# Seven-product FFN blocks: weight buffers, token order of the out projection, and the order of first tiles and products

## Chip, cores and metric

One core of one Trainium2 chip. The metric is the device time of one execution in microseconds (us), the median of several. TensorE is called PE here, VectorE DVE, ScalarE ACT, GpSimd POOL and SyncE SP.

## The reference

One decoder layer over 2048 prompt tokens and 64 sample tokens (8 sequences of 8), width 1024. What matters here is its second half:

```python
    mix = jnp.concatenate([oa, ob, oc, od], axis=-1).astype(dt) @ prm['w_out'][li]
    h = h + mix
    gu = rmsnorm(h, prm['norm2_g'][li]) @ prm['w_ffn_in'][li]
    h = h + (jax.nn.silu(gu[..., :D_FF]) * gu[..., D_FF:]) @ prm['w_ffn_out'][li]
    gate = jax.nn.sigmoid(rmsnorm(h, prm['ple_norm_g'][li]) @ prm['w_ple_gate'][li])
    h = h + (pl @ prm['w_ple'][li]) * gate
```

`D_FF` is 2816. `oa` to `od` are four token mixers (linear attention, dilated attention, gated delta rule, recurrent gates).

## The kernel before

The tokens are worked on in four blocks of 512 (`TB`); the 64 sample tokens ride with block 1 through the input projection and with block 3 through the rest, which then has 576 columns (`TBS`). A block has tiles 0 to 3 of 128 tokens; tile 4 is the 64 sample tokens, and the order of tiles is 0, 1, 4, 2, 3. Every product is done with operands split in two, a rounded part `hi` and a remainder `lo`, and three matmuls (hi hi, hi lo, lo hi) per 128 rows of contraction. A weight is loaded by SP into `wraw` (4 buffers), `hi` is cast on ACT into `whi` (7 buffers) and `lo` subtracted on DVE or POOL into `wlo` (7 buffers); `unit`, line 268 on, does this and alternates DVE and POOL.

Blocks 0 and 1 use `rest`, blocks 2 and 3 use `rest7` (line 596). `rest7` does the out projection (`out_mm`, line 434: four column quarters of 256, for each of them the tiles in turn), then `norm2`, then the FFN in `ffn7`, then the per-layer part (`per_layer_out`). The FFN runs over 22 row groups f of 128. Of a group, gate and up are computed together by a scheme of seven products of half the contraction, each over half of the block's tokens (256 columns, or 288 in block 3), instead of eight; `seven` (line 680) builds sums of weights on DVE, splits them (`parts`, lines 691 and 692), runs the products (`prod`, line 715) into three PSUM banks x, y and z, and combines them with DVE additions (line 696). The seven products are a11, s1, s2, a12, s3, s4, a22. The token operands are b11 and b21 (first half of the tokens), b22, and the differences t1 to t4; `Halves.steps` (line 121) transposes the normalized rows on PE (line 134), copies them out of PSUM scaled (`F`, lines 139 and 141) and splits the first half; `Halves.second` (line 153) makes the differences (line 164) and their splits. The first group, f = 0, is done by eight products, `mm_half` (line 670), half by half, since its first half needs only the first half of the tokens. FFN groups go in chunks of 1, 3, 3, ..., 3; after each chunk `out_mm` multiplies its gated values `g` with `w_ffn_out` (line 364, 512 columns) and adds to the residual rows `h` (line 582). The last chunk goes tile by tile, with the last norm's transposes (line 85) between.

The order of instructions on each engine is worked out when the kernel is built: a scheduler takes whatever is ready by its own modelled times, in order of a priority that counts up with the program text; `S.at(0)` puts something ahead of everything else. The sample tokens' mixers are given a higher priority than block 2 of `rest7` and run beside it. Pools of a new stage lie on memory of closed ones and wait tile by tile for it to come free. There are two pools of three PSUM banks for these products (`bank`), taken in turn.

## Time and profile before

| | us |
|---|---|
| median of three runs | 3446.8 |
| lowest and highest run | 3443.35, 3446.89 |
| profiled execution | 3437.55 |
| its span, first to last instruction | 3435.7 |
| PE busy in it | 3302.0 |
| DVE busy in it | 2254.7 |
| granted PE clock, mean | 0.978 |

The profile is of one execution. A row of the windows has, after the stretch and its length, the busy time (and instructions) of PE, its weight loads (PEld), DVE, ACT and POOL, then the granted clock as a share of full speed. Block 2's out projection ends in the stretch from 2346 to 2396 us, block 3's in that from 2910 to 2960, and block 3's work ends the span. A matmul's recorded time includes its way through the array, so the distance between starts is what one costs.

### The profile page before, as it was taken

Reading aid. Unit: us, or ns where it says so; the run is one execution under the profiler, and the core shown is the slowest. Engines: PE = TensorE matmul, PEld = TensorE weight load, DVE = VectorE, ACT = ScalarE, POOL = GpSimd, SP = SyncE. Lnnn points to the kernel's source line nnn. Section 1 sums busy time; section 2 is a strip of 40 time slices with the busy share of each in tenths; the row PEclk is TensorE's granted clock in tenths of the full one; section 3 lists DMA queues with packets and bytes.
Section 4 is the critical chain, followed back from the end, with each engine's and each line's share of the span. In section 5 each row is a group of like instructions: output and inputs, shape, how many; then the busy total and the mean of one; then the engine's idle time right before and its main releaser. Section 6 shows DMA issues by size and latency. Waiting matters only on the chain.

```text
span 3435.7 us, 66579 instructions
## 1 busy us (share of the span) xinstructions
PE 3302.0 (96%) x24742; PEld 2815.2 (82%) x24742; DVE 2254.7 (66%) x6002; ACT 1379.3 (40%) x2931; POOL 820.7 (24%) x696
## 2 busy tenths in 40 slices
PE   7999999999999999998999999999999999899998
PEld 6788997888887778788878776787888889788988
DVE  4455566544577756688775455446799875877875
ACT  4433445324344224345333334535343453433443
POOL 2212122122112222212122212122334432233431
PEclk9999999999999999999999999999999999999999
DMA  6645445544433332534432443463533344122222
GB/s 207 181 121 149 127 123 155 148 125 145 129 109 118 101 96 87 132 91 146 113 103 81 124 114 110 143 215 113 162 102 88 91 129 134 60 81 90 83 89 79
DMA packets 621769, 411.92 MB, mean 120 GB/s; under 512 B 155357, under 2 KB 572877, under 8 KB 621445
## 3 DMA queue, kind: packets, MB, share of 16 engines
q1 hardware_dynamic: 618184, 405.12, 40.8%
q8 instruction: 195, 3.19, 0.4%
q10 hardware_dynamic: 3260, 2.55, 0.3%
q14 instruction: 130, 1.06, 0.1%
HBM read 348.77 MB, written 61.18 MB: 119 GB/s over the span
## 4 chain that ended last, share of the span: by engine, by line
PE 72%; DVE 13%; DMA 6%; SPq 4%; issue 3%; ACT 2%; POOL 1%; DVEq 0%; ACTq 0%; POOLq 0%
PE mmp L364 25%; PE mmp L344 22%; PE mmp L715 9%; SPq L1321 2%; PE acc L1852 1%; DVE c_X L1312 1%; DVE c_tmp L1310 1%; DMA wraw<-w_ffn_in 1%; DVE wlo L283 1%; PE mx L1135 1%; PE mx L1707 1%; PE mmp L85 1%; PE mx L1653 1%; PE mx L1764 1%; PE mx L1047 1%
## 5 line engine op out<-in xcount | busy, mean ns | idle before, releaser
L283 POOL TENSOR_TENSOR wlo<-wraw,whi 128x512 fp32r<-128x512 f32 (+1 forms) x356 | 497.5, 1399 | 1763.0 <-ACT whi L280 1112.8
L344 PE MATMUL mmp<-act,whi 128*128 128x512 f32 (+1 forms) x2944 | 892.7, 384 | 7.6 <-ACT ev L368 5.0
L280 ACT CAST whi<-wraw 128x512 fp32r<-128x512 f32 (+1 forms) x712 | 436.4, 619 | 667.4 <-PE mmp L344 240.6
L344 PEld LDWEIGHTS mmp<-act,whi 128*128 128x128 f32 x2944 | 532.9, 190 | 111.9 <-ACT ev L368 6.8
L364 PE MATMUL mmp<-whi,act 128*128 128x256 f32 (+3 forms) x2992 | 574.8, 290 | 11.8 <-DVE act L297 6.9
L344 PE MATMUL mmp<-act,wlo 128*128 128x512 f32 (+1 forms) x1472 | 554.0, 383 | 0.0
L364 PE MATMUL mmp<-whi,g 128*128 128x512 f32 (+1 forms) x1496 | 491.2, 406 | 15.4 <-DVE h L492 5.8
L364 PEld LDWEIGHTS mmp<-whi,act 128*128 128x128 f32 (+1 forms) x2992 | 470.8, 190 | 21.5 <-DVE act L297 7.8
L364 PE MATMUL mmp<-wlo,act 128*128 128x256 f32 (+2 forms) x1496 | 431.0, 289 | 0.2 <-DVE wlo L283 0.2
L283 DVE TENSOR_TENSOR wlo<-wraw,whi 128x512 fp32r<-128x512 f32 (+1 forms) x356 | 279.9, 787 | 219.0 <-ACT whi L280 198.3
L692 POOL TENSOR_TENSOR wlo<-wraw,whi 128x512 fp32r<-128x512 f32 x168 | 243.6, 1453 | 468.6 <-ACT whi L691 411.8
L364 PEld LDWEIGHTS mmp<-whi,g 128*128 128x128 f32 (+1 forms) x1496 | 273.3, 188 | 95.5 <-ACT g L296 8.5
L715 PE MATMUL mmp<-Sb,whi 128*128 128x256 f32 (+1 forms) x1680 | 328.0, 292 | 7.2 <-DVE xs L696 5.8
L344 PEld LDWEIGHTS mmp<-act,wlo 128*128 128x128 f32 x1472 | 276.4, 190 | 50.2 <-issue 2.0
L364 PE MATMUL mmp<-wlo,g 128*128 128x512 f32 x748 | 297.6, 400 | 0.0
L364 PEld LDWEIGHTS mmp<-wlo,act 128*128 128x128 f32 (+1 forms) x1496 | 283.5, 190 | 4.0 <-issue 2.0
L715 PEld LDWEIGHTS mmp<-Sb,whi 128*128 128x128 f32 x1680 | 267.0, 190 | 12.7 <-DVE xs L696 8.4
L715 PE MATMUL mmp<-Sb,wlo 128*128 128x256 f32 (+1 forms) x840 | 241.7, 291 | 1.8 <-POOL wlo L692 1.8
L691 ACT CAST whi<-wraw 128x512 fp32r<-128x512 f32 x210 | 128.8, 619 | 229.1 <-PE mmp L364 94.5
L364 PEld LDWEIGHTS mmp<-wlo,g 128*128 128x128 f32 x748 | 140.2, 187 | 33.7 <-issue 0.5
L715 PEld LDWEIGHTS mmp<-Sb,wlo 128*128 128x128 f32 x840 | 159.0, 190 | 3.4 <-POOL wlo L692 2.2
L582 DVE TENSOR_TENSOR h<-mmp,h 128x512 f32<-128x512 f32 (+3 forms) x180 | 107.6, 630 | 72.0 <-PE mmp L364 65.5
(472 smaller groups left out, 5250.1 us busy)
## 6 DMA issues: line engine op xcount, KB each, us to landing
wraw<-w_ffn_in SPq DMA_DIRECT2D x352, 256.0 KB
wraw<-w_in SPq DMA_DIRECT2D x208, 256.0 KB
wraw<-w_ffn_out SPq DMA_DIRECT2D x176, 256.0 KB
wraw<-w_out SPq DMA_DIRECT2D x64, 256.0 KB
wraw<-w_ple_gate SPq DMA_DIRECT2D x64, 256.0 KB
bs_K<-cache_b_k SPq DMA_DIRECT2D x48, 256.0 KB
...
```

What stands on the lines that cost most here:

```text
L85: nc.tensor.transpose(ps[:, i * rows:(i + 1) * rows], s[:, k * 128:(k + 1) * 128], S.ident[:rows, :rows])
L280: nc.scalar.copy(hi, raw)
L283: eng.tensor_tensor(lo, raw, hi.bitcast(F32), op=ALU.subtract)
L344: nc.tensor.matmul(ps, u[a], acts[k][:, b, t:t + w], start=i == 0, stop=i == n)
L364: nc.tensor.matmul(ps, acts[k][:, b, t0:t0 + rows], units[k][a], start=i == 0, stop=i == n)
L582: nc.vector.tensor_tensor(d, ps, d, op=ALU.add)
L691: nc.scalar.copy(hi, x)
L692: eng.tensor_tensor(lo, x, hi.bitcast(F32), op=ALU.subtract)
L715: nc.tensor.matmul(ps, w[a][:, k], op[k][:, b], start=first and k == 0 and j == 0, stop=k == 3 and j == 2, skip_group_check=True)
L1047: nc.tensor.matmul(ss[:, k:k + 2], x[:, c, t * m:(t + 1) * m], M.blk2, start=True, stop=True)
L1135: nc.tensor.matmul(ps[64 * hp:64 * hp + ms, ct, n], k[r, ct, 64 * n:64 * n + ms], part(q[r, ct, 64 * n:64 * n + 64], 1), start=True, stop= ...
L1321: nc.sync.dma_start(out=xt[r, ct, n], in_=xd[:, hp, ct, n, d].rearrange("k j i -> j k i"))
```

## The change

In words, by function:

- `Halves`: the tokens lie in the order of the tiles, 0, 1, samples, 2, 3, so one copy instead of two takes a transposed group out of PSUM; half of these copies (k of 4 and more) go to DVE. The second group's transposes get the priority of their place in the text instead of the top one. `second` splits b12 and b22 of all k before it makes differences; the splits of t3 go to POOL. `F` shares its buffers with half of the differences (`Sf`).
- Weight parts come from further pools in turn with the old ones (`wparts`): 7 more in block 3, in the out projection and in the FFN each, 3 more in block 2's FFN. Sums of weights (`ws`) get 5 buffers in block 2.
- `out_mm` in block 3's out projection (`late`): the last two column quarters are done for tiles 0, 1 and 4 first, then both for tiles 2 and 3, with two steps of the norm after each of these products. `mid` gives the tiles their new place.
- `ffn7`: f = 0 and f = 1 are both done by halves, in the order first half of 0, second group of the norm, first half of 1, second half of 0, second half of 1. The chunks are 2, 3, 3, 3, 3, 3, 3, 2. The gated values are split in one piece.
- `seven`: the split of s1 comes later, s2 is split on DVE and a12 on POOL; the products go a11, s2, a12, s1, s3, s4, a22.

```diff
+    ORDER = (0, 4, 1, 5, 2, 6, 3, 7)
...
-        self.f = [fp.tile([128, 2 * self.w], F32, name="F") for _ in range(KT)]
+        self.f = {k: sf.tile([128, 2 * self.w], F32, name="F", tag="Sb") for k in self.ORDER}
...
-            for k in (0, 4, 1, 5, 2, 6, 3, 7):
-                with S.at(0):
+            for k in self.ORDER:
+                with S.at(S.tc.cur_priority if j else 0):
...
-                    t0 = j * w
-                    m = w if n > 256 else 256
-                    nc.scalar.mul(f[:, t0:t0 + m], ps[:, :m], g)
-                    if n > m:
-                        nc.scalar.mul(f[:, 2 * w - n + m:], ps[:, m:], g)
+                    g, f = self.gain[:, k:k + 1], self.f[k][:, t0:t0 + n]
+                    if k < 4:
+                        nc.scalar.mul(f, ps, g)
+                    else:
+                        nc.vector.tensor_scalar_mul(f, ps, g)
...
+            t0 += n
...
+        new = lambda p: p.tile([128, 2, w], F32R, name="Sb", tag="Sb")
+        for k in range(4):
+            S.split(self.b12[k], self.part(k, 1))
+            self.b22.append(new(sb))
+            S.split(self.b22[k], self.part(k + 4, 1))
         for k in range(4):
             b11, b12, b21, b22 = (self.part(a, j) for a, j in ((k, 0), (k, 1), (k + 4, 0), (k + 4, 1)))
-            d = sb.tile([128, 2, self.w], F32R, name="Sb")
-            self.b22.append(d)
-            S.split(d, b22)
             tmp = S.xsp.tile([128, D], F32, name="xs")
-            t1, t2, t3 = (tmp[:, i * self.w:(i + 1) * self.w] for i in range(3))
+            t1, t2, t3 = (tmp[:, i * w:(i + 1) * w] for i in range(3))
             sub(t1, b12, b11)
+            sub(t2, b22, t1)
             sub(t3, b22, b12)
-            sub(t2, b22, t1)
-            S.split(self.b12[k], b12)
-            sub(b21, b21, t2)
-            for n, x in (("t1", t1), ("t2", t2), ("t3", t3), ("t4", b21)):
-                d = sb.tile([128, 2, self.w], F32R, name="Sb")
-                self.t[n].append(d)
-                S.split(d, x)
+            for n, x in (("t1", t1), ("t2", t2), ("t3", t3), ("t4", t1)):
+                if n == "t4":
+                    sub(x, b21, t2)
+                self.t[n].append(new(sb if k < 2 else self.sf))
+                S.split(self.t[n][k], x, nc.gpsimd if n == "t3" else None)
...
+    def wparts(self):
+        self.nw += 1
+        _, hi, lo = self.wpools[self.nw % len(self.wpools)]
+        return hi, lo
...
+        hi, lo = self.wparts()
+        hi = hi.tile([128, nk, n], F32R, name="whi", tag="whi")
+        lo = lo.tile([128, nk, n], F32R, name="wlo", tag="wlo")
...
-            nc.vector.tensor_tensor(lo, src, hi.bitcast(F32), op=ALU.subtract)
+            (eng or nc.vector).tensor_tensor(lo, src, hi.bitcast(F32), op=ALU.subtract)
...
+        elif late:
+            def pairs():
+                for c in cols[:-2]:
+                    u = load(c)
+                    yield from ((c, i, u) for i in tiles)
+                us = [(c, load(c)) for c in cols[-2:]]
+                for part in (tiles[:-2], tiles[-2:]):
+                    yield from ((c, i, u) for c, u in us for i in part)
+            order = pairs()
...
-            use(i, c, self.mm_a(acts, u, nk, i * 128, NS if i == 4 else 128, n))
+            t0 = i * 128 if not mid or i < 2 else 256 if i == 4 else i * 128 + NS
+            use(i, c, self.mm_a(acts, u, nk, t0, NS if i == 4 else 128, n))
...
+            if late:
+                if not left[tiles[-3]] and i in tiles[-2:]:
+                    for _ in range(2):
+                        if steps < 8:
+                            norm.step()
+                            steps += 1
+            elif norm and not left[tiles[2]]:
...
-            ws, fp, sa = (ops.enter_context(pool(n, m)) for n, m in (("ws", 2), ("F", KT), ("Sa", KT)))
-            with pool("pad", 1) as pad, pool("W", KT) as wp:
-                if not with_s:
-                    pad.tile([128, 1400], F32, name="pad")
+            ws, sa, sf = (ops.enter_context(pool(n, m)) for n, m in (("ws", 2 if with_s else 5), ("Sa", KT), ("Sf", KT)))
+            @contextmanager
+            def weights(n):
+                with pool("whi2", n) as hi, pool("wlo2", n) as lo:
+                    own = self.wpools
+                    self.wpools = own + (own if n < 7 else []) + [(None, hi, lo)]
+                    yield
+                    self.wpools = own
+            with pool("W", KT) as wp, weights(7) if with_s else nullcontext():
                 self.actps, self.nacts = [wp], 0
                 acts = self.mixed(mix, smix)
                 for i, _ in self.tiles(with_s):
                     h[i] = self.load_x(self.hp.tile([128, D], F32, name="h"), b, i)
-                norm = Halves(self, h, self.gain["norm2_g"], with_s, fp, sa)
-                self.out_mm(acts, I["w_out"][0], KT, 256, with_s, add, norm)
-            last = self.ffn7(add, norm, ops.enter_context(pool("Sb", 20)), ws, with_s, w0)
+                norm = Halves(self, h, self.gain["norm2_g"], with_s, sa, sf)
+                self.out_mm(acts, I["w_out"][0], KT, 256, with_s, add, norm, late=with_s)
...
+            sb = ops.enter_context(pool("Sb", 12))
+            ops.enter_context(weights(7 if with_s else 3))
+            last = self.ffn7(add, norm, sb, ws, with_s)
...
+                self.out_mm(*last, 512, with_s, add, norm, True, mid=with_s)
...
+        def bank2(n):
+            if 2 * w0 > TB:
+                return [self.bank()[:, :w0] for _ in range(n)]
+            t = [self.bank() for _ in range((n + 1) // 2)]
+            return [t[i // 2][:, i % 2 * w0:(i % 2 + 1) * w0] for i in range(n)]
+        def glu(pairs):
+            th = self.ev.tile([128, TBS], F32, name="ev")
+            for j, (gate, up) in enumerate(pairs):
+                e = th[:, j * w0:(j + 1) * w0]
+                nc.scalar.activation(e, gate, AF.Tanh, scale=0.5)
+                nc.vector.scalar_tensor_tensor(e, e, 1.0, gate, op0=ALU.add, op1=ALU.mult)
+                nc.vector.scalar_tensor_tensor(e, e, 0.5, up, op0=ALU.mult, op1=ALU.mult)
+            g = self.gp.tile([128, 2, 2 * w0], F32R, name="g", tag="g")
+            self.split(g, th[:, :2 * w0])
+            return g
...
+        for n in (2, 3, 3, 3, 3, 3, 3, 2):
             gs = []
-            for f in range(f0, f0 + n):
-                wg, wu = (wi[:, c0:c0 + 128] for c0 in (f * 128, D_FF + f * 128))
-                th = self.ev.tile([128, TBS], F32, name="ev")
-                if f:
-                    pairs = self.seven(wg, wu, ops, ws, w0)
-                else:
-                    us = [self.units([w], KT, 4) for w in (wg, wu)]
-                    norm.first()
-                    pairs = []
-                    for j in range(2):
-                        if j:
-                            norm.second(sb)
-                        if w0 == 256:
-                            t = self.bank()
-                            ps = [t[:, :w0], t[:, w0:]]
-                        else:
-                            ps = [self.bank()[:, :w0] for _ in us]
-                        pairs.append([self.mm_half(p, u, norm.half(j)) for p, u in zip(ps, us)])
-                    ops = norm.operands(sb)
-                for j, (gate, up) in enumerate(pairs):
-                    e = th[:, j * w0:(j + 1) * w0]
-                    nc.scalar.activation(e, gate, AF.Tanh, scale=0.5)
-                    nc.vector.scalar_tensor_tensor(e, e, 1.0, gate, op0=ALU.add, op1=ALU.mult)
-                    nc.vector.scalar_tensor_tensor(e, e, 0.5, up, op0=ALU.mult, op1=ALU.mult)
-                g = self.gp.tile([128, 2, 2 * w0], F32R, name="g", tag="g")
-                gs.append(g)
-                halves = th[:, :2 * w0].rearrange("p (j n) -> p j n", j=2)
-                for c, m in ((0, 256), (256, w0 - 256)):
-                    if m:
-                        self.split(g[:, :, 2 * c:2 * (c + m)].rearrange("p a (j n) -> p a j n", j=2),
-                                   halves[:, :, c:c + m])
+            if not f0:
+                us = [[self.units([w], KT, 4) for w in cols(f)] for f in range(n)]
+                norm.first()
+                half = lambda f, j: [self.mm_half(ps, w, norm.half(j)) for ps, w in zip(bank2(2), us[f])]
+                pairs = [[half(0, 0)], []]
+                norm.second(sb)
+                pairs[1].append(half(1, 0))
+                for f in range(2):
+                    pairs[f].append(half(f, 1))
+                gs = [glu(p) for p in pairs]
+                ops = norm.operands()
+            gs += [glu(self.seven(*cols(f), ops, ws, w0)) for f in range(f0 + len(gs), f0 + n)]
             w = wo[f0 * 128:(f0 + n) * 128]
             f0 += n
             if f0 < FT:
-                self.out_mm(gs, w, n, 512, with_s, add)
+                self.out_mm(gs, w, n, 512, with_s, add, mid=with_s)
...
-        s1 = parts(s, V)
         tt(u1, g1, u1)
         tt(g1, s, g1)
-        s2 = parts(g1, G)
-        a12 = parts(g2, V)
+        s2 = parts(g1, V)
+        a12 = parts(g2, G)
+        s1 = parts(s, V)
...
-        x, z, y = (self.bank()[:, :w0] for _ in range(3))
+        x, y, z = (self.bank()[:, :w0] for _ in range(3))
         sv = self.xsp.tile([128, D], F32, name="xs")
         s, v, u = (sv[:, i * w0:(i + 1) * w0] for i in range(3))
         prod(x, a11, ops["b11"], True)
         nc.scalar.copy(s, x)
-        prod(z, s1, ops["t1"], True)
-        tt(v, z, s, ALU.add)
         prod(y, s2, ops["t2"], True)
         tt(u, y, s, ALU.add)
         prod(x, a12, ops["b21"], False)
+        prod(z, s1, ops["t1"], True)
+        tt(v, z, s, ALU.add)
```

## Rows read from the trace of the kernel before

**Rows 1.** The page's first part: busy time, share of the span and instructions of each engine.
```profile
PE 3302.0 (96%) x24742; PEld 2815.2 (82%) x24742; DVE 2254.7 (66%) x6002; ACT 1379.3 (40%) x2931; POOL 820.7 (24%) x696
```
**Rows 2.** Windows over stages: length, busy by engine, granted clock, DMA share, GB/s.
```profile
2346.00:2396.00 50.00, 42.89 (x382) 34.10 (x383) 37.22 (x100) 33.93 (x79) 5.90 (x4) 0.93 0.35 102
2396.00:2740.00 344.00, 328.68 (x2484) 288.07 (x2483) 289.42 (x600) 140.11 (x282) 136.53 (x97) 0.99 0.40 111
...
2910.00:2960.00 50.00, 37.20 (x222) 32.23 (x221) 44.06 (x118) 29.18 (x76) 6.35 (x5) 0.83 0.11 32
2960.00:3340.00 380.00, 376.22 (x2363) 337.68 (x2363) 293.84 (x460) 149.72 (x295) 143.24 (x103) 1.00 0.29 88
```
**Rows 3.** Windows over undisturbed matmuls of 288, 512 and 256 columns.
```profile
2961.00:2989.00 28.00, 28.00 (x213) 28.00 (x212) 22.54 (x38) 14.76 (x30) 14.26 (x11) 1.00 0.33 101
2999.50:3013.50 14.00, 13.85 (x60) 10.37 (x60) 9.90 (x16) 3.01 (x6) 3.68 (x3) 1.00 0.14 39
2810.00:2905.00 95.00, 94.86 (x804) 94.66 (x803) 49.13 (x114) 32.09 (x71) 22.78 (x16) 1.00 0.43 136
```
**Rows 4.** PE's waits, 2910 to 2960 us: total us, times, longest.
```profile
PE mmp L364 <- ACT g L296: 2.9, 1, 2.9
PE mmp L134 <- DVE xs L68: 2.8, 1, 2.8
PE mmp L676 <- DVE Sb L297: 2.8, 1, 2.8
PE mmp L134 <- ACT F L141: 2.7, 2, 2.5
```
**Rows 5.** Windows of 20 us in block 3's hand-over, columns as in the windows above.
```profile
2920.00:2940.00 20.00, 14.10 (x89) 13.07 (x90) 18.07 (x53) 15.41 (x46) 0.00 (x0) 0.74 0.05 14
2940.00:2960.00 20.00, 14.35 (x65) 11.43 (x64) 17.15 (x36) 6.76 (x16) 3.43 (x3) 0.83 0.14 39
```
**Rows 6.** Timeline, tile 3's rows from residual add to scaling: start us, us, engine.
```profile
2918.16 0.41 DVE L582 TENSOR_TENSOR h<-mmp,h 128x256 f32<-128x256 f32 x1
...
2922.55 1.14 ACT L313 ACTIVATE xs<-h 128x1024 f32<-128x1024 f32 x1
...
2927.51 0.75 DVE L68 TENSOR_SCALAR xs<-h,ss 128x1024 f32<-128x1024 f32 x1
```
**Rows 7.** Groups by line and shape, 2910 to 2960: busy us, mean ns | idle before.
```profile
L139 ACT ACTIVATE F<-mmp,gcol 128x288 f32<-128x288 f32 x8 | 3.7, 531 | 0.0
L164 DVE TENSOR_TENSOR xs<-F 128x288 f32<-128x288 f32 x8 | 3.5, 460 | 1.4 <-ACT F L139 1.4
```
**Rows 8.** PE's waits in block 2's FFN, 2396 to 2740 us.
```profile
PE mmp L715 <- DVE xs L696: 4.1, 7, 1.7
PE mmp L715 <- POOL wlo L692: 1.8, 2, 1.1
```
**Rows 9.** DVE's groups by line and shape in block 3's FFN, 2960 to 3340.
```profile
L696 DVE TENSOR_TENSOR ws<-wraw 128x512 f32<-128x512 f32 x39 | 47.3, 1214 | 18.3 <-DMA wraw<-w_ffn_in 18.1
L696 DVE TENSOR_TENSOR xs<-mmp,xs 128x288 f32<-128x288 f32 x105 | 46.1, 449 | 22.9 <-PE mmp L715 22.5
...
L696 DVE TENSOR_TENSOR wraw<-ws,wraw 128x512 f32<-128x512 f32 x20 | 13.6, 682 | 2.3 <-POOL wlo L692 2.2
...
L297 DVE TENSOR_TENSOR g<-ev,g 128x64 fp32r<-128x64 f32 x21 | 4.5, 213 | 0.0
```
**Rows 10.** PE's waits in block 3's FFN, 2960 to 3340.
```profile
PE mmp L364 <- DVE g L297: 1.9, 5, 0.4
...
PE mmp L715 <- DVE xs L696: 0.3, 1, 0.3
```
**Rows 11.** PE's waits at block 2's tail, 2770 to 2810.
```profile
PE mmp L85 <- DVE h L582: 3.2, 4, 1.7
PE mmp L364 <- DVE act L300: 1.6, 2, 1.4
```
**Rows 12.** POOL's group of weight splits, 2396 to 3340.
```profile
L692 POOL TENSOR_TENSOR wlo<-wraw,whi 128x512 fp32r<-128x512 f32 x165 | 239.0, 1452 | 441.4 <-ACT whi L691 384.6 <-PE mmp L364 23.5 <-PE mmp L715 23.4
```

45 lines of the change are left out of this document (19 added, 26 removed).

## Prediction

> **What bounds the kernel now.** I read the page's busy shares first: TensorE (PE) is busy 96% of the span [rows 1], so time can only come from stretches where PE waits or runs at the low clock, or from matmuls saved. The change touches only the two token blocks done with seven products (block 2 and block 3, `rest7`), so next come the windows over that part [rows 2]: block 2's hand-over from out projection to FFN (2346 to 2396 us), its FFN beside the sample mixers (2396 to 2740), block 3's hand-over (2910 to 2960) and block 3's FFN (2960 to 3340). The hand-over of block 3 sticks out: PE is busy 37.2 of 50 us there, at a granted clock of 0.83 on average, while the FFN after it has PE busy 376.2 of 380 at full clock. Third, the windows over undisturbed stretches give what a matmul costs when nothing is in its way [rows 3]: 804 in 95 us, 0.118 us each, for 256 columns; 213 in 28 us, 0.1315, for 288; 60 in 14 us, 0.233, for 512. Fourth, the list of PE's waits in the hand-over [rows 4] and the granted clock in its two 20 us slices [rows 5]: 0.74 and 0.83, a mix of the levels 2.4 and 1.2 GHz; the clock fell after PE had idled in the normalization and again after it had waited for `Sb` and `g`. In those slices VectorE (DVE) is busy 18.1 and 17.2 of 20 us: it is what PE waits for, directly or through ScalarE (ACT).
>
> **How much is lost there.** PE's work in 2910 to 2960 by the code and the prices: two out products, 48 x 0.118 = 5.7; the four halves of f = 0, 96 x 0.1315 = 12.6; the chunk of one f, 30 x 0.233 = 7.0; about 36 transposes of 128 columns, under the price of 256, some 3.5; the start of the next seven, 0.8. Sum 29.6 of 50: 20.4 us lost, idle and slow clock together.
>
> **The change part by part.** Durations are of the profiled execution, 3437.55 us (span 3435.7 and 1.9 around it); the median shown, 3446.8, lies 9.2 above it, and I add that at the end.
>
> *Block 3's hand-over.* Two edits act. `late` puts the last two column quarters of tiles 2 and 3 behind everything of tiles 0, 1 and 4, so once the first group's rows are final, four products (4 x 24 x 0.118 = 11.3 us) still run instead of two (5.7). And f = 1 is computed by halves too, so that 24 x 2 more matmuls on the first half (6.3 us) stand between the first half's operands and the second half's; the second group's transposes lose their top priority and no longer stand ahead of the halves. Count from the end T of tile 4's last product. The rows of tile 4 need a residual add, a square, a root and a scaling: tile 3 took 10.1 us for it, of which the square stood some 4 us behind other work in ACT's queue [rows 6], so about 6 free. Then eight times: one copy out of PSUM (0.53 us [rows 7]; ACT for four, DVE for four, where ACT now does all eight and eight more of 32 columns, which go) and a split in two, on ACT at most the copy's 0.53, on DVE 0.46 (the price of a 288 column operation there [rows 7]): 6.4 us on ACT, 5.8 on DVE, side by side. Operands at T + 12.5; PE is through its four products and 24 transposes at T + 13.3. So the 2.8 and 2.7 us of waiting there [rows 4], the shorter ones beside them and the slow clock behind them go. What is late next is the second group: tile 3's rows are ready 6 us after T + 13.3, just as the first half of f = 0 ends (T + 19.6). Then 1.5 us of transposes and three halves of 6.3 end at T + 40.4. DVE has to do by then, at 0.46 for 288 columns and 0.68 for 512 [rows 7, 9]: four copies, 8 splits, 16 differences, 12 splits, the gates of two f (about 5) and the next weights (7 x 0.68): about 28 by durations, rather less because they overlap at their ends, against PE's 27. It just fits, so I leave 5 us of loss (between 0 and 11, the upper end being the waits on `Sb` and `g` as now, 5.7 us, and the slow clock they cause). Gain 15.4, between 9 and 20.
>
> *Twelve more matmuls per block.* Halves cost 96 matmuls, a seven 84: 12 x 0.1315 + 12 x 0.118 = 3.0 us more, all on PE's path. The DVE operations that the seven of f = 1 no longer needs lie in DVE's full stretch and are in the count above.
>
> *Block 2's hand-over.* No `late` here; the windows give 7.1 us idle and 0.07 x 50 = 3.5 of slow clock, about 10 us [rows 2], and the matmuls of the sample mixers, which have a higher priority, already fill part of it. Gained are the second f (5.7 us of cover) and the lower priority of the second group; that priority now also lets sample work go ahead of it. I take 4 saved, between 8 saved and 2 lost.
>
> *The last chunk has two f instead of three* (the first two instead of one). It is the cover for the last norm: block 2 has 8 x 3 x 0.233 = 5.6 us less of it, block 3 7.0. In block 2 PE already waits 4.8 us there for the residual add and the splits [rows 11], so this cover is used up: I take 3 us more. The list of waits over block 3's tail is empty: nothing, 1.5 if its cover is gone. Term +3, between 0 and 7.
>
> *More buffers for weight parts* (10 in block 2, 14 in block 3, against 7). In block 2 PE waits in the sevens for a DVE combination out of PSUM 4.1 us and for a POOL part 1.8 us [rows 8]; DVE is busy 289 of 344 us [rows 2]. Buffers let DVE and ACT run further ahead, but the raw weights still have four buffers, one f's worth, and DVE's work does not shrink. I take 2 saved, between 6 saved and 5 lost (reordering costs something where DVE is this full). In the out projection of block 3 they are needed for `late` and hide nothing.
> The Trainium skill (Perfetto Trace Analysis, Optimization Strategy) says that the same gap repeating on the engine that should be full can mean too few buffers. By it all 5.9 us would go and the forecast would be 4 us lower; the rows name a DVE combination, not a weight part, for most of it, and do not bear the rule out.
>
> *Block 3's FFN.* 3.8 us idle in 380 [rows 2], 1.9 of it for the DVE half of `g` [rows 10]. The new token order makes the split of `g` one operation instead of two: 21 x 0.21 us on DVE [rows 9] and as many on ACT go, in front of each chunk's first matmul. I take 1.5 saved, between 4 saved and 4 lost (the product order, below).
>
> *Other engines.* The second differences' `t3` splits and the split of `a12` go to POOL, `s2` comes to DVE; POOL is busy 137 of 344 us [rows 2], and a 512 column split takes it 1.45 us [rows 12]. DVE's two-input operation on raw weights takes 1.21 us on average, another of the same size 0.68 [rows 9].
> The Trainium skill (SBUF — State Buffer, "SBUF: two separate sides") says why: DVE with two SBUF inputs and POOL lock one port pair for a whole instruction. By it the four `t3` splits take about 4 x 0.8 us of DVE's time away (an estimate, 288/512 of 1.45) and give back 4 x 0.46, so the hand-over would gain 1.5 less; the two durations agree with it.
>
> **Sum:** -15.4 + 3.0 - 4 + 3 - 2 - 1.5 = -16.9 us. 3437.55 becomes 3420.7 in such an execution, and the median 3446.8 becomes 3430.
>
> **The rivals.** *The hand-over stays bound by DVE* (3440). For it: DVE is 90% and 86% busy now [rows 5] and gets four copies more; with 288 columns each half takes two PSUM banks, six banks hold three halves, so the last half waits until the gate arithmetic of the first has been squeezed in between the differences. Against: f = 1's halves are cover that was not there. Then the hand-over gains 5 instead of 15.4: -6.5.
> *The order is not what the text says* (3442). The order on each engine is worked out when the kernel is built, from modelled times, and the new weight buffers of the FFN lie in memory of the out projection's operands, so that the first f's weights in them can only be split after its last product (0.68 to 1.45 us after a cast, before a half can go on [rows 9, 12]). The hand-over then gains about 3.5: -5.
> *The sevens' stalls go as well* (3420). If looking further ahead unties DVE's queue, most of the idle in block 2's FFN that lies in sevens, some 10 of the 15.3 us [rows 2], goes, and block 2's hand-over with it.
> *Slower: the new product order* (3454). In a seven, x takes its second product (a12) after one other product instead of two, and must wait for ACT's copy of x; z takes s4 after one product instead of three and must wait for DVE's v; only y's second gets more room. One product is 12 x 0.118 = 1.4 us in block 2, 1.6 in block 3; DVE's combination takes 0.45 [rows 9] and may stand behind an operation of 1.21: 1.66. If every one of 40 sevens then lost 0.6 us, the mean of the seven waits in block 2 [rows 8], that is 24 us and the sum +7. It decides at 17/40 = 0.42 us a seven. Against it: two accumulations already have cover of one product, and block 3 shows a single wait of 0.3 us in 21 sevens [rows 10], block 2 4.1 us in 18.
>
> **How the numbers follow.** Forecast 0.50, stalls gone too 0.17, DVE-bound hand-over 0.15, order 0.07, product order 0.11. The ends of the terms, added as independent, give 3421 to 3443 for the forecast alone; with the rivals at 3420 and 3442 and the spread of the three runs (3.5 us) 3417 to 3446, which leaves out the slower case and the tails. 0.2%, about what a measurement of this kernel can tell from no change, is 6.9 us: faster than 3439.9 are the forecast nearly whole, the bigger gain and half of the DVE-bound case, 0.72; within it 0.16; slower 0.12.
>
> **What would show it.** Right: in block 3, between the out projection's last product and the first seven, no PE wait above 2 us and no slice below clock 0.95; the stretch from tile 4's last product to the end of the first chunk about 15 us shorter after allowing for the second f; block 3's FFN still about 99% busy; per block 84 fewer matmuls of the sevens and 96 more of the halves. The DVE case would show PE waiting for `Sb` or a PSUM bank before the last half; the product order, waits on ACT's copy or on `xs` in every seven; the tail, longer waits for the residual add before block 2's last transposes. The prediction is wrong if the out projection of block 3 becomes slower through `late`, which I cost at nothing because its weights wait for nobody now (804 matmuls in 95 us [rows 3]).

## The result and the profile after

The changed kernel takes 3468.4 us (median of 4 runs) against 3445.1 for the kernel before beside it: ratio 1.0069, 95% interval 1.0052 to 1.0087. I had forecast 3430; it is slower, by the mechanism to which I had given 0.11, and by others that I had not seen. The profiled execution takes 3468.98 us, its span is 3467.2, 31.5 more than in the one of before, which lay below its own median.

From the page of the changed kernel: the busy line, and from the chain that ended last its shares by engine and by line.

```profile
PE 3319.2 (96%) x24766; PEld 2828.2 (82%) x24766; DVE 2221.9 (64%) x5968; ACT 1363.3 (39%) x2877; POOL 824.5 (24%) x700
...
PE 68%; DVE 13%; DMA 9%; SPq 4%; issue 3%; ACT 2%; POOL 1%; DVEq 0%; ACTq 0%; POOLq 0%
PE mmp L353 23%; PE mmp L373 23%; PE mmp L749 5%; DMA wraw<-w_ffn_in 3%; SPq L1355 2%; PE acc L1886 1%; PE mmp L709 1%; DVE c_tmp L1344 1%; DVE c_X L1346 1%; DVE wlo L292 1%; DMA wraw<-w_ffn_out 1%; PE mx L1741 1%; DVE wraw L730 1%; PE mx L1169 1%; PE mmp L85 1%
```

Matmuls rose by 24 against [rows 1], as counted. On the chain the sevens (L749) hold 5% and the load of raw weights 3%, against 9% and 1% on the page of before: the FFN now waits more for its weights. Windows of the changed kernel by stage (length, busy of each engine, granted clock, DMA share, GB/s): block 2's hand-over, FFN and tail, block 3's out projection, hand-over and FFN, which answer to [rows 2].

```profile
2346.60:2413.10 66.50, 61.29 (x520) 51.08 (x519) 46.46 (x110) 38.93 (x85) 20.42 (x14) 0.92 0.39 116
2413.10:2790.10 377.00, 352.28 (x2600) 307.45 (x2599) 297.73 (x621) 145.87 (x296) 139.49 (x103) 0.97 0.38 107
2790.10:2826.30 36.20, 29.19 (x174) 25.24 (x172) 28.20 (x86) 20.21 (x49) 4.84 (x4) 0.91 0.40 132
2826.30:2926.90 100.60, 97.15 (x806) 96.53 (x805) 50.16 (x135) 35.15 (x78) 18.73 (x14) 0.98 0.42 132
2926.90:3000.70 73.80, 61.38 (x392) 54.72 (x391) 61.40 (x133) 32.49 (x75) 29.29 (x17) 0.91 0.20 58
3000.70:3359.10 358.40, 350.36 (x2198) 317.35 (x2197) 249.51 (x401) 133.08 (x246) 131.36 (x94) 0.99 0.28 85
```

The lengths of such stages can't be compared as they stand, since the work in them moved. So I compare what is *lost* in a stage: its length less the time that its matmuls take at undisturbed spacing (the prices of [rows 3]; small shapes by their spacing in the undisturbed parts of the trace of before). It holds idle time and slow clock together. The level of block 2's columns depends on how the sample mixers' small matmuls are priced, so read differences there. All kernels below have the same order of instructions up to block 2's hand-over, which began at 2340 to 2358 us in their profiled executions; that spread is the executions', and the stages are compared behind it. The ratios are of the runs, each with its 95% interval.

| kernel | ratio to before | block 2 hand-over | block 2 FFN | block 2 tail | block 3 out projection and hand-over | block 3 FFN | DVE waits for raw weights, block 3 FFN |
|---|---|---|---|---|---|---|---|
| before | 1 | 19.0 | 56.1 | 7.9 | 20.8 | 10.0 | 18.1 |
| changed | 1.0069 (1.0052 to 1.0087) | 18.9 | 69.8 | 11.0 | 24.8 | 15.7 | 37.2 |
| e1 old sevens | 1.0038 (1.0026 to 1.0050) | 18.6 | 58.4 | 8.4 | 23.5 | 9.1 | 23.9 |
| e2 few buffers | 1.0051 (1.0039 to 1.0063) | 17.5 | 64.4 | 11.2 | 15.9 | 17.6 | 51.7 |
| e3 half first | 1.0048 (1.0032 to 1.0064) | 12.4 | 63.7 | 13.0 | 21.5 | 13.3 | |
| e4 half first, weights free | 1.0038 (1.0023 to 1.0052) | 12.4 | 62.9 | 12.1 | 17.4 | 15.3 | |
| e5 old products only | 1.0062 (1.0048 to 1.0077) | 19.2 | 67.1 | 8.6 | 25.0 | 14.0 | 31.8 |
| e6 before, new sevens | 1.0049 (1.0035 to 1.0063) | 18.5 | 61.6 | 9.3 | 21.6 | 14.3 | 40.3 |
| e7 no late | 1.0081 (1.0064 to 1.0098) | 19.0 | 65.7 | 12.0 | 21.3 | 15.7 | |
| e8 combination | 0.9953 (0.9937 to 0.9968) | 10.9 | 53.1 | 8.2 | 8.1 | 9.8 | 26.7 |
| e9 own tile for s4 | 1.0058 (1.0045 to 1.0070) | 17.9 | 59.9 | 12.4 | 24.8 | 10.9 | 29.1 |
| e10 old parts only | 1.0059 (1.0044 to 1.0073) | 18.9 | 63.7 | 10.3 | 23.6 | 15.7 | 37.7 |
| e11 e8 without late | 0.9975 (0.9965 to 0.9984) | 12.4 | 54.2 | 8.9 | 17.4 | 9.6 | 24.2 |
| e12 e8 with buffers | 1.0009 (0.9998 to 1.0019) | 13.0 | 62.3 | 8.1 | 19.4 | 9.1 | 24.3 |
| e13 e8 with new sevens | 1.0002 (0.9991 to 1.0014) | 10.9 | 61.6 | 11.0 | 10.0 | 22.0 | 53.5 |
| e14 e8, one f by halves | 1.0027 (1.0018 to 1.0036) | 8.7 | 78.5 | 8.1 | 9.0 | 22.5 | 25.9 |
| e15 e8, sample load early | 0.9940 (0.9926 to 0.9954) | 12.1 | 54.3 | 7.4 | 5.8 | 10.2 | |

Two things limit how finely this table can be read. First, each stage is read from one execution. The changed kernel and e7 have the same order of PE instructions in block 2, and so have e3 and e4, and e8 and e15: block 2's FFN reads 69.8 and 65.7, 63.7 and 62.9, 53.1 and 54.3. So a difference of 4 us in that column can be nothing but the execution's.

Second, the changed kernel was run only in the first comparison, four times. The kernel before had a median of 3445.1 us beside it, but 3436.9 to 3439.5 in the five later comparisons (9 to 23 runs each, on four chips). Set against those, 3468.4 would be 1.0084 to 1.0092, at the upper end of its interval or just beyond, and every gain over the changed kernel that is read from the ratios would be 5 to 8 us larger. By the medians themselves e1 lies 18.9 us below the changed kernel, e2 14.3, e4 17.5, e5 8.9, e9 9.6, e10 10.4 and e8 48.5. The stages go with the medians: added up over the table's five columns of losses, e1 is 22.2 us below, e2 13.6, e4 20.1 and e8 50.1. So where gains over the changed kernel are compared below, both are given.

The first two rows say where 31.5 us went: block 2's FFN 13.7, its tail 3.1, block 3's out projection and hand-over 4.0, its FFN 5.7, its tail 2.0, and 3.1 for 24 more matmuls. The hand-over, from which I expected 15.4, gained 0.7 (18.9 to 18.2 lost), and the out projection ahead of it lost 4.7 more.

### What the hand-over does in the changed kernel

Its waits of PE (total us, times, longest), which answer to [rows 4]:

```profile
PE mmp L137 <- DVE ss L327: 7.2, 1, 7.2
PE mmp L137 <- DVE xs L68: 2.0, 1, 2.0
PE mmp L373 <- DVE ev L674: 1.2, 1, 1.2
```

The timeline of PE, from the out projection's last product to the first half (start us, us, engine, instruction, idle before):

```profile
2941.85 0.28 PE L373 MATMUL mmp<-wlo,act 128*128 128x256 f32 x1
2949.30 1.54 PE L137 MATMUL mmp<-ident,xs 128*128 128x128 f32 x6 [7.17 <-DVE ss L327]
2952.82 2.17 PE L137 MATMUL mmp<-ident,xs 128*128 128x128 f32 x8 [1.99 <-DVE xs L68]
...
2956.13 0.85 PE L709 MATMUL mmp<-Sa,whi 128*128 128x288 f32 x2
```

The second group's transposes (L137 on tiles 2 and 3) still stand ahead of the first half (L709), which needs the first group alone. The same stretch on ACT, POOL and DVE:

```profile
2941.79 2.18 ACT L289 CAST whi<-wraw 128x512 fp32r<-128x512 f32 x4
2943.87 1.06 ACT L322 ACTIVATE xs<-h 128x1024 f32<-128x1024 f32 x1
...
2942.54 5.45 POOL L292 TENSOR_TENSOR wlo<-wraw,whi 128x512 fp32r<-128x512 f32 x4 [49.70 <-ACT whi L289]
...
2942.51 1.90 DVE L306 TENSOR_TENSOR Sa<-F,Sa 128x288 fp32r<-128x288 f32 x2
2944.33 1.23 DVE L334 SCALAR_TENSOR_TENSOR ss<-ss 128x1 f32<-128x1 f32 x1
2945.59 1.19 DVE L333 SCALAR_TENSOR_TENSOR ss<-ss 128x1 f32<-128x1 f32 x1
2946.81 1.19 DVE L334 SCALAR_TENSOR_TENSOR ss<-ss 128x1 f32<-128x1 f32 x1
...
2949.16 0.15 DVE L327 TENSOR_SCALAR ss<-ss 128x1 f32<-128x1 f32 x1
```

Four weight parts are cast only as the out projection's last product runs; the casts go ahead of tile 3's square on ACT, and four splits run back to back on POOL. Meanwhile DVE's root of tile 2, operations on one column, takes 1.2 us a step. The granted clock fell to 0.50, 1.2 GHz, at 2946.4, within PE's 7.2 us of idling, and came back at 2960.0.

### The profile page after: what moved, and what is told of

It reads as the page before. It is cut to its first block, busy times and chain, and to the rows that moved or that the text cites. A ratio compares the mean times of both kernels' runs of the same rounds, so it can differ in the third digit from the quotient of the medians.

```text
span 3467.2 us, 66394 instructions
## 1 busy us (share of the span) xinstructions
PE 3319.2 (96%) x24766; PEld 2828.2 (82%) x24766; DVE 2221.9 (64%) x5968; ACT 1363.3 (39%) x2877; POOL 824.5 (24%) x700
## 3 DMA queue, kind: packets, MB, share of 16 engines
q1 hardware_dynamic: 618184, 405.12, 40.4%
## 4 chain that ended last, share of the span: by engine, by line
PE 68%; DVE 13%; DMA 9%; SPq 4%; issue 3%; ACT 2%; POOL 1%; DVEq 0%; ACTq 0%; POOLq 0%
PE mmp L353 23%; PE mmp L373 23%; PE mmp L749 5%; DMA wraw<-w_ffn_in 3%; SPq L1355 2%; PE acc L1886 1%; PE mmp L709 1%; DVE c_tmp L1344 1%; DVE c_X L1346 1%; DVE wlo L292 1%; DMA wraw<-w_ffn_out 1%; PE mx L1741 1%; DVE wraw L730 1%; PE mx L1169 1%; PE mmp L85 1%
## 5 line engine op out<-in xcount | busy, mean ns | idle before, releaser
L373 PE MATMUL mmp<-whi,act 128*128 128x256 f32 (+3 forms) x2992 | 578.9, 291 | 19.0 <-DVE act L306 7.1
L373 PE MATMUL mmp<-whi,g 128*128 128x512 f32 (+1 forms) x1496 | 499.5, 412 | 25.4 <-DVE xs L730 12.0
L373 PEld LDWEIGHTS mmp<-whi,act 128*128 128x128 f32 (+1 forms) x2992 | 473.1, 191 | 28.9 <-DVE act L306 7.9
L373 PE MATMUL mmp<-wlo,act 128*128 128x256 f32 (+2 forms) x1496 | 432.3, 290 | 1.7 <-DVE wlo L292 1.7
L373 PEld LDWEIGHTS mmp<-whi,g 128*128 128x128 f32 (+1 forms) x1496 | 277.6, 191 | 103.6 <-DVE xs L730 16.7
L726 POOL TENSOR_TENSOR wlo<-wraw,whi 128x512 fp32r<-128x512 f32 x160 | 234.3, 1473 | 430.1 <-ACT whi L725 339.6
L749 PE MATMUL mmp<-Sb,whi 128*128 128x256 f32 (+1 forms) x1600 | 314.4, 291 | 9.1 <-DVE xs L730 8.8
L373 PE MATMUL mmp<-wlo,g 128*128 128x512 f32 (+1 forms) x748 | 301.4, 404 | 0.0
L373 PEld LDWEIGHTS mmp<-wlo,act 128*128 128x128 f32 (+1 forms) x1496 | 284.6, 190 | 5.9 <-DVE wlo L292 2.2
L749 PEld LDWEIGHTS mmp<-Sb,whi 128*128 128x128 f32 x1600 | 254.8, 190 | 18.3 <-DVE xs L730 14.3
L749 PE MATMUL mmp<-Sb,wlo 128*128 128x256 f32 (+1 forms) x800 | 230.7, 290 | 0.0
L725 ACT CAST whi<-wraw 128x512 fp32r<-128x512 f32 x200 | 121.3, 619 | 194.2 <-PE mmp L373 71.7
L373 PEld LDWEIGHTS mmp<-wlo,g 128*128 128x128 f32 (+1 forms) x748 | 141.8, 190 | 33.9 <-issue 0.2
L749 PEld LDWEIGHTS mmp<-Sb,wlo 128*128 128x128 f32 x800 | 151.3, 190 | 1.0 <-issue 0.8
```

The costliest lines, as they stand in the source:

```text
L373: nc.tensor.matmul(ps, acts[k][:, b, t0:t0 + rows], units[k][a], start=i == 0, stop=i == n)
L725: nc.scalar.copy(hi, x)
L726: eng.tensor_tensor(lo, x, hi.bitcast(F32), op=ALU.subtract)
L749: nc.tensor.matmul(ps, w[a][:, k], op[k][:, b], start=first and k == 0 and j == 0, stop=k == 3 and j == 2, skip_group_check=True)
```

## The experiments

**e1, e5, e10 and e6: the order of the sevens.** e1 puts both hunks of `seven` back in the changed kernel; e5 only the products (`prod`), e10 only the parts; e6 puts both new hunks into the kernel before.

```diff
+        s1 = parts(s, V)
         tt(u1, g1, u1)
         tt(g1, s, g1)
-        s2 = parts(g1, V)
-        a12 = parts(g2, G)
-        s1 = parts(s, V)
+        s2 = parts(g1, G)
+        a12 = parts(g2, V)
...
+        prod(z, s1, ops["t1"], True)
+        tt(v, z, s, ALU.add)
         prod(y, s2, ops["t2"], True)
         tt(u, y, s, ALU.add)
         prod(x, a12, ops["b21"], False)
-        prod(z, s1, ops["t1"], True)
-        tt(v, z, s, ALU.add)
```

> The changed kernel with one part undone: in the sevens the order of the products (a11, s1, s2, a12, s3, ...) and of the weight parts, and the engine of each part, are those of the kernel before; all other edits stay. Theory A (product order): the 13.8 us that TensorE loses more in block 2's FFN and the 5.7 us in block 3's come from x and z taking their second products sooner; they come back: about 19 us below the changed kernel's 3468, 3449, ratio 1.001. Theory B (run-ahead): what costs is that the new weight buffers let VectorE take the weight sums of the next f, and their wait for the raw weights, ahead of the combinations; with the old seven the losses stay: 3464 to 3470, ratio 1.006. Theory C (the order of the out products, bunched behind the third f): as B, no change.

Measured 1.0038: 0.3% back by the ratios (10.7 us; 18.9 by the medians), and in the stages 11.4 us of block 2's FFN, 6.6 of block 3's and 4.9 in the two tails. Theory A stands against B and C. Waits in block 3's FFN, of the changed kernel:

```profile
PE mmp L373 <- DVE xs L730: 6.9, 6, 2.2
...
DVE ws L730 <- DMA wraw<-w_ffn_in: 37.2, 17, 4.1
```

and of e1:

```profile
DVE ws L730 <- DMA wraw<-w_ffn_in: 23.9, 17, 2.0
...
PE mmp L373 <- DVE xs L730: 0.3, 1, 0.3
```

How the two hang together shows at a chunk's start in the changed kernel, timeline of DVE and then PE:

```profile
3036.34 0.45 DVE L730 TENSOR_TENSOR xs<-mmp,xs 128x288 f32<-128x288 f32 x1
3039.63 0.69 DVE L730 TENSOR_TENSOR ws<-wraw 128x512 f32<-128x512 f32 x1 [2.84 <-DMA wraw<-w_ffn_in]
3040.24 0.45 DVE L674 SCALAR_TENSOR_TENSOR ev<-ev,xs 128x288 f32<-128x288 f32 x1
3040.61 0.69 DVE L730 TENSOR_TENSOR wraw<-wraw 128x512 f32<-128x512 f32 x1
...
3041.57 0.45 DVE L730 TENSOR_TENSOR xs<-mmp,xs 128x288 f32<-128x288 f32 x1
...
3043.26 0.76 DVE L306 TENSOR_TENSOR g<-ev,g 128x576 fp32r<-128x576 f32 x1 [0.74 <-ACT g L305]
...
3042.08 0.73 PE L373 MATMUL mmp<-whi,g 128*128 128x512 f32 x2 [0.85 <-DVE xs L730]
```

The last product ended before 3038; its combination (3041.57) and the gate chain stand in DVE's queue behind the next f's sum u1 + u2, which waits 2.84 us for raw weights. PE waits 0.85 us in front of an out product until that combination has ended.

> The changed kernel with one part undone: only the order of the seven products on TensorE is that of the kernel before; the order of the weight parts and the engine of each stay as changed. The run with both undone gave back 11 to 14 us in block 2's FFN and 7 in block 3's. Theory A1 (the product order alone costs this: x and z must take their second product one product after ScalarE's copy or VectorE's combination): the same comes back here, ratio 1.0035 to 1.0045. Theory A2 (the weight parts: s1's low half comes last of its batch on VectorE, a12's went to GpSimd and s2's to VectorE): nothing comes back or it gets worse, ratio 1.0065 or more, since z now takes s1 as second product while its part is made fourth.

> The changed kernel with one part undone: order and engines of the weight parts as before; the products in the changed order. The run with only the products undone gave little back. Theory A2 or F (the weight parts carry the cost): block 2's FFN loses 58 to 62 us and block 3's 9 to 12, ratio 1.0035 to 1.0045. Theory A1 (the product order): no gain, 1.006 or more. A mix (both, and it is the mismatch of parts and products that costs): 1.005 to 1.006.

Measured 1.0062 and 1.0059. The products alone cure the tails (8.6 and 1.8 us lost against 11.0 and 4.2), the parts alone bring block 2's FFN to 63.7. Neither A1 nor A2 holds, since neither half gives back all. By the ratios the halves give back 0.1% each and both together 0.3%, as if parts and products had to fit each other; by the medians they give back 8.9 and 10.4 us, which add up to e1's 18.9. That they have to fit each other is not shown.

> The kernel before with one part of the change alone: the sevens of the changed kernel (products and weight parts); weight buffers, first tiles, out projection and chunks as before. Theory A (the sevens' order costs by itself): block 2's FFN loses 10 to 14 us more, block 3's 4 to 7 and the tails 2 to 5: 16 to 24 us, ratio 1.005 to 1.007. Theory B (it costs only together with the new buffers, which let VectorE run ahead): within 5 us of the kernel before, ratio 0.999 to 1.0015.

Measured 1.0049, 0.0001 short of the range that A gave: 17 us, with 5.5 more lost in block 2's FFN (A had said 10 to 14), 4.3 in block 3's and 3.1 in the tails. The order costs by itself.

**e9: why the raw weights come late.** In the changed kernel the last sum, g2 - g1, no longer overwrites the tile of u1 + u2:

```diff
-        tt(s, g2, g1)
+        s = ws.tile([128, 4, 128], F32, name="ws"); tt(s, g2, g1)
```

> The changed kernel with one line different: the sum g2 - g1 of the seven is written into a ws tile of its own instead of over the tile of u1 + u2 (the pool stays at 2 in block 3 and 5 in block 2). Theory F (release of the raw weights): in the changed order s1 is the fourth of seven parts, and the sum that overwrites its tile and frees the raw g1 and g2 stands behind its split, which waits for TensorE to free a weight buffer; so the raw weights of the next f are ordered later, VectorE waits for them (37 us over block 3's FFN instead of 18) with the gate chain queued behind. With its own tile the waits on the raw weights in block 3's FFN fall to 18 to 25 us, TensorE's loss in the FFNs falls by 8 to 19 us, ratio 1.002 to 1.0045. Rival G (it is the number of operations in front of the gate chain or GpSimd's work, not the tile): the waits stay above 30 us and the ratio at 1.006 to 1.007.

The waits on raw weights fell to 29.1, between the two, and the FFNs lost 9.9 and 4.8 us less; but the time fell by 0.1% by the ratios, within the intervals (9.6 us by the medians), about half of what undoing the order gives, or less. The step that frees the raw weights has a part in it; that it is the cause isn't shown.

**e2: the extra buffers.** The changed kernel without the FFN's second pools:

```diff
-            ops.enter_context(weights(7 if with_s else 3))
```

> The changed kernel with one part undone: no second pair of weight-part pools in the FFNs of blocks 2 and 3 (7 buffers again, as before; the pools beside block 3's out projection stay). Theory B (run-ahead): VectorE can no longer run ahead, its waits for raw weights in block 3's FFN (38 us) go back towards 18, and 10 to 19 us come back: 3449 to 3458, ratio 1.001 to 1.004. Theory A (product order): no gain, 3466 to 3472. If the buffers do help, as I had forecast, the time grows by 2 us or more.

Measured 1.0051, 6 us below the changed kernel by the ratios and 14.3 by the medians. The gain lies elsewhere than B put it: 8.9 us in block 3's out projection and hand-over, 5.4 in block 2's FFN, and the waits on raw weights rose to 51.7. So B is right that the buffers hurt and wrong on how.

**e3 and e4: the hand-over as I had predicted it.** e3 leaves out one line, so that the second group follows the first half; e4 also chooses the pools of block 3's parts by hand (0 the first, 1 the second): of `late`'s eight held parts all but one in the second, the FFN's first six in the first and the next two in the second (the expectation says seven).

```diff
-                norm.first()
...
+                self.force = [0, 1] * 4 + [1] * 7 + [0] * 7 + [1] * 2 if with_s else []
...
-        _, hi, lo = self.wpools[self.nw % len(self.wpools)]
+        i = self.force.pop(0) if self.force else self.nw
+        _, hi, lo = self.wpools[i % len(self.wpools)]
```

> The changed kernel with one line less: norm.first() is not called at the head of the FFN, so that the second group's transposes stand behind the first half of f = 0 in the text and in TensorE's order; nothing is left out. Theory D (transposes in front): in block 3's hand-over the 7.2 us wait of TensorE for the root operations of tile 2 goes, since the first half needs only the first group; but the first f's weights are still split only behind the out projection's end, on GpSimd four in a row, so some 3 to 4 us of waiting for wlo stay: 4 to 6 us less than the changed kernel, 3463, ratio 1.0055. Rival E (VectorE-bound hand-over): VectorE's work of about 28 us sets its end whatever TensorE does first: within 2 us of the changed kernel, 3467 to 3470.

> The changed kernel with the second group's transposes behind the first half (as in the run before) and, in block 3, the eight weight parts that the late columns hold taken from the second pair of pools but for one, so that the first seven parts of the FFN have free buffers and can be split beside the out projection. This is the hand-over as my prediction had it. Theory D: both obstacles are gone, TensorE goes from the out projection to the first half without a wait over 1 us, and the stretch loses about 5 instead of 18 us: 13 us below the changed kernel, 3455, ratio 1.003. Rival E (VectorE-bound): TensorE waits before the second halves instead, 12 us or more stay lost, 3464 to 3469.

Measured 1.0048 and 1.0038. Block 2's hand-over lost 6.5 us less in both. In block 3, e3 lost 3.3 less and e4 7.4, not 13. In e4 PE goes from the out projection into the first half without a wait (last out product at 2927.28, first half at 2927.39); what is left are waits behind it. The longest of PE's waits in e4's hand-over:

```profile
PE mmp L373 <- DVE g L306: 2.6, 1, 2.6
```

In e3 the wait for `g` in front of this out product (L373) is 6.1 us. So D's two obstacles were real, and half of E too: a third thing was left, which e8 and e12 show.

**e8 and e12: all together, with and without the extra buffers.** e8 is the changed kernel with the diffs of e1, e2 and e4; e12 is e8 without that of e2.

> The changed kernel with four things together: the sevens of the kernel before, the second group's transposes behind the first half, the FFNs with 7 weight buffers, and the late columns' parts in the second pools but one, so that seven parts of the FFN can be made beside block 3's out projection. If the separate gains add (sevens 11 us by the medians, halves first with weights 11, buffers 6): 28 us below the changed kernel, 3440 against 3468, ratio 0.9985, 0.996 at best. Rival: the gains are the same stall taken away twice (halves first and buffers both cure the first f's weights), ratio 1.000 to 1.001.

> The combination that ran at 0.9953, with the second weight pools of the FFNs given back (10 buffers in block 2, 14 in block 3). If the buffers only hurt together with the new order of the parts: FFNs lose the same (53 and 10 us) or up to 3 us less, ratio 0.9945 to 0.9955. If they hurt by themselves (VectorE runs ahead): block 2's FFN loses 5 us more, ratio 0.9965 to 0.9975.

Measured 0.9953 and 1.0009. e8 is the first kernel that beats both. By the ratios it lies 12 us below what the single gains of e1, e2 and e4 add up to; but by the medians they add up to 50.7 us against e8's 48.5, and by the table's columns to 55.9 against 50.1. More than their sum is not shown. Its hand-over and FFN of block 3, windows:

```profile
2898.00:2956.00 58.00, 56.76 (x391) 52.00 (x390) 50.60 (x127) 27.34 (x64) 17.30 (x10) 1.00 0.14 42
2956.00:3308.50 352.50, 348.95 (x2197) 313.82 (x2196) 258.19 (x407) 136.69 (x252) 135.46 (x97) 1.00 0.30 88
```

The hand-over is at full clock with one PE wait (1.2 us for `g`) and loses 2.5 us. With the buffers back (e12) block 2's FFN loses 9.2 more and block 3's out projection and hand-over 11.3 more, about the 19 us between the ratios. The timeline of e12 on ACT, DVE and PE behind the out projection shows what free buffers do in block 3:

```profile
2924.66 2.19 ACT L289 CAST whi<-wraw 128x512 fp32r<-128x512 f32 x4 [0.16 <-PE mmp L373]
2926.75 1.06 ACT L322 ACTIVATE xs<-h 128x1024 f32<-128x1024 f32 x1
...
2925.92 1.80 DVE L292 TENSOR_TENSOR wlo<-wraw,whi 128x512 fp32r<-128x512 f32 x1
2927.65 1.26 DVE L333 SCALAR_TENSOR_TENSOR ss<-ss 128x1 f32<-128x1 f32 x1
2928.83 0.68 DVE L292 TENSOR_TENSOR wlo<-wraw,whi 128x512 fp32r<-128x512 f32 x1
...
2935.82 1.97 PE L137 MATMUL mmp<-ident,xs 128*128 128x128 f32 x8 [1.32 <-DVE xs L68]
```

And the same place on ACT in e8:

```profile
2913.26 0.63 ACT L289 CAST whi<-wraw 128x512 fp32r<-128x512 f32 x1 [0.17 <-PE mmp L373]
2913.83 1.06 ACT L322 ACTIVATE xs<-h 128x1024 f32<-128x1024 f32 x1
```

The last out product's final matmul starts at 2924.46 in e12 and at 2913.06 in e8. A buffer that is free lets the build put weight parts that nobody needs yet in front of the norm's square and root, and each engine works in the order that was built. With 7 buffers one cast stands there and the square begins 0.8 us after that matmul; with 14 there are four casts, and it begins 2.3 us after it. That the buffers cost 19 us is shown by the two runs; how 1.5 us here grow to 11.3, and what happens in block 2's FFN, isn't followed.

**e13: the sevens' order without the extra buffers.** e8 without the diff of e1.

> The combination that ran at 0.9953 (no second weight pools in the FFNs, second group's transposes behind the first half, the first seven parts of block 3's FFN in free buffers), but with the changed order of the sevens. Theory A (the order costs by itself): as in the kernel before, 0.4 to 0.5% more, ratio 0.9995 to 1.001, with block 2's FFN losing 60 us or more against 53 and block 3's 14 or more against 10. Theory H (it is the extra buffers that let weight work run ahead on ScalarE and VectorE, and the order only adds to that): ratio 0.995 to 0.997.

Measured 1.0002, 17 us above e8: A again, with block 2's FFN at 61.6 and block 3's at 22.0. Its waits in block 3's FFN:

```profile
DVE ws L730 <- DMA wraw<-w_ffn_in: 53.5, 19, 5.8
...
PE mmp L749 <- DVE xs L730: 9.7, 11, 2.0
PE mmp L373 <- DVE xs L730: 2.3, 3, 1.3
```

The table's last two columns go together over twelve of the kernels: where DVE waits up to 27 us for raw weights the FFN loses 9 to 10 us, at 29 to 32 it loses 11 to 14, at 37 and more 14 to 22. (e14's stage begins earlier and holds part of the hand-over.)

**e14: the second f by halves.** e8 with f = 1 by a seven:

```diff
-                us = [[self.units([w], KT, 4) for w in cols(f)] for f in range(n)]
+                us = [[self.units([w], KT, 4) for w in cols(f)] for f in range(1)]
...
-                pairs = [[half(0, 0)], []]
+                pairs = [[half(0, 0)]]
                 norm.second(sb)
-                pairs[1].append(half(1, 0))
-                for f in range(2):
-                    pairs[f].append(half(f, 1))
+                pairs[0].append(half(0, 1))
```

> The combination that ran at 0.9953, with f = 1 computed by a seven again, as in the kernel before (chunks stay at 2, 3, ..., 3, 2). My prediction's step (the second f by halves is 6 us of cover a block in front of the second halves and costs 3.0 us of matmuls): 6.1 us of matmuls go, and in each block some 5 to 8 us of waiting come in front of the second half and of the first seven, which needs all the second operands: ratio 0.9965 to 0.998. Rival (VectorE and ScalarE keep up without it, as the hand-over of the combination shows no waits): only the 6.1 us of matmuls go, ratio 0.9935.

Measured 1.0027, 25 us above e8, though it has 24 matmuls less (3.0 us by the prediction's term; the expectation counts them twice). Its first sevens of block 3 begin amid the second halves, and from there to the FFN's end PE waits:

```profile
PE mmp L749 <- DVE xs L730: 3.9, 2, 2.7
...
PE mmp L709 <- DVE g L306: 1.5, 3, 0.8
```

Hand-over and FFN together lose 14 us more in block 3 and 23 in block 2, in an execution that was its slowest, 10 us above its median. By the ratios the cover is worth some 14 us a block (25 and the 3 of matmuls saved, over two blocks), more than the 6 that I had counted.

**e7 and e11: `late`.** The last columns not parted, in the changed kernel and in e8 (there the last column's four parts in the second pools, the FFN's first eight in the first):

```diff
-                self.out_mm(acts, I["w_out"][0], KT, 256, with_s, add, norm, late=with_s)
+                self.out_mm(acts, I["w_out"][0], KT, 256, with_s, add, norm)
```

> The changed kernel with one part undone: block 3's out projection goes column by column over all tiles, as before (the pools beside it stay). Theory D (late gives 5.7 us of cover, but holds eight weight parts): the 3 us wait for a weight part two thirds through the out projection goes and with it the slow clock behind it, 4.8 us in all; the hand-over stays at about 18 us lost, since what it waits for (tile 2's root, the first f's weights) is later than the cover: the sum of out projection and hand-over loses 19 to 21 instead of 24.8, ratio 1.0055. My prediction's step (late is cover): 4.8 come back and 5.7 more are lost, ratio 1.007.

> The combination that ran at 0.9953, without the late columns: block 3's out projection column by column over all tiles, the last column's parts in the second pools, the FFN's first seven in the first. My prediction's step (late gives two products, 5.7 us, of cover in front of the first half): the hand-over, which now waits for nothing else, loses 5 to 6 us more, ratio 0.997. Theory D (late's own cost, a wait of 3 us for a weight part and a slow clock behind it, about equals its cover): 0.9945 to 0.9960.

e7: 1.0081, not told from the changed kernel. Out projection and hand-over lose 21.3, near D's sum, but the wait that D put down to late's weight parts is still there (2.3 us), so that part of D falls. e11: 0.9975, 7.6 us above e8, with 9.3 more lost in out projection and hand-over: once nothing else holds the hand-over, late's cover counts, as my step had it (5.7).

**e15: the wait in the out projection.** Its operand is `act`, not a weight part. PE's longest wait in the changed kernel's out projection:

```profile
PE mmp L373 <- ACT act L305: 2.7, 1, 2.7
```

ACT's own wait for that load, then SP's queue and PE there:

```profile
ACT act L305 <- DMA ev<-mixs_a: 3.0, 1, 3.0
```

```profile
2865.50 8.97 SPq L287 DMA_DIRECT2D wraw<-w_out  x5
...
2881.62 1.30 SPq L287 DMA_DIRECT2D wraw<-w_out  x2
2882.97 0.55 SPq L647 DMA_DIRECT2D ev<-mixs_a  x1
...
2888.21 0.83 PE L373 MATMUL mmp<-whi,act 128*64 128x256 f32 x3 [2.66 <-ACT act L305]
```

It is the first product of tile 4: the sample tokens' mixer outputs are ordered on SP behind ten loads of `w_out` and land after PE needs them. Before, seven such loads stood ahead of them in the stretch that I looked at, and PE didn't wait. That the second pools admit the further ones is my reading. e15 is e8 with

```diff
-            ms = self.ev.tile([128, TBS], F32, name="ev")[:, :KT * NS].rearrange("p (k n) -> p k n", k=KT)
+            ms = self.xsp.tile([128, D], F32, name="xs")[:, :KT * NS].rearrange("p (k n) -> p k n", k=KT)
```

> The combination that ran at 0.9953, with one line different: the sample tokens' mixer outputs are loaded into an xs tile instead of an ev tile, so that the load is issued before the loads of the out projection's weights and not behind ten of them. If this load is the cause of the 2.9 us wait of TensorE at the out projection's first product of tile 4, the wait goes and with it the slow clock behind it: the out projection loses 1 to 2 us instead of 5.6, ratio 0.994. If the wait moves to something else (the prompt tokens' outputs, which use the same tiles, come later), the out projection loses 4 us or more and the ratio stays at 0.995.

Measured 0.9940 (median 3418.3, the lowest). Out projection and hand-over lose 5.8 instead of 8.1; of the wait some moved on to the prompt tokens' operands:

```profile
PE mmp L373 <- DVE act L309: 2.4, 2, 2.0
PE mmp L373 <- DVE h L607: 1.6, 2, 1.5
```

Less than expected comes back, and e15 and e8 can't be told apart by their intervals; that the wait on this load goes is shown, that all of it is gained is not.

## Why the prediction was wrong, point by point

**Block 3's hand-over (-15.4; measured -0.7).** The step that failed is "the second group's transposes lose their top priority and no longer stand ahead of the halves". They lose the priority, but the text itself has them in front: `out_mm` takes the eight steps of the first group and `norm.first()` eight more, which are the second. I read the priority and not the count of steps. (By its own terms the sum of that stretch ends at T + 40.0, not 40.4; nothing hangs on it.) The sum also went from the operands' time alone and left the first f's weights out, which I had only as a rival with 0.07. The size was right: with order and buffers mended, e8 loses 2.5 where before lost 18.9, 16.4 less. Its two halves were not: late's cover is worth 8 to 9 us (e11), the second f far more than its 6 (e14); that the sum agrees is in part luck.

**Buffers (-2; measured about +19).** The difference of e12 and e8; taken out of the changed kernel (e2) they give back 6 us by the ratios, 14 by the medians. I let DVE and ACT "run further ahead" as a gain and did not ask what stands behind work that runs ahead. Rows [rows 8] named a combination, not a weight part, for 4.1 of the 5.9 us, so buffers could gain little there, and the bound of +5 was set without a row. The Trainium skill (Perfetto Trace Analysis, Optimization Strategy) says that repeating gaps can mean too few buffers; that was not the case here: e12, with more buffers, loses more in the same stages (9.2 us in block 2's FFN).

**The sevens (in the block 3 FFN term, -1.5; and the slower rival, 0.11).** The rival was right that the order costs: it turned the balance at 0.42 us a seven, and the 17 us of e6 and e13 are 0.40 over 42 sevens and 0.42 over 40, part of them in the tails. The waits are not in every seven, as the rival had it: in block 3's FFN of the changed kernel PE waits in front of the out products (6.9 us) more than in the sevens (1.2 us). What I set against it, one product of cover, goes by PE's clock alone; where the delay was followed, it comes from DVE's queue, where the combination stands behind a sum that waits for raw weights. [rows 9] had that wait, 18.1 us before the change, and I read it as nobody's loss. Why the new order makes the weights later, and how much of the loss that explains, stays open (e9).

**Tails (+3; measured +5.1), right in sign by a wrong step.** I put it down to two f of cover instead of three. e1, e5, e8 and e14 have two f and lose as little as before (8.1 to 8.6 in block 2); there it was the order of the products (e5). Block 3's 2.0 is not settled: e13 has the new sevens and loses 1.9 in all.

**Twelve more matmuls a block (+3.0; 24 counted on the page, 3.1 us by their prices).** Right, and worth it (e14).

**Block 2's hand-over (-4; measured -0.1).** The same misread order: without `norm.first()` it loses 6.5 us less (e3, e4), 8.1 less in e8.

**"Wrong if the out projection becomes slower through `late`".** It is 4.7 us slower, but not through `late` (in e7 the wait stays): the 2.7 us wait, and the slow clock of 2888 to 2892 behind it, come from a load queued behind weights on SP, a queue that I hadn't walked. e15 gets 2.3 us back with it; the rest is open.
